# First block of a two-block network: decay rows by one product, small copies and half of the low weight parts on GpSimd, the solver's two problems joint, beta at the tokens

## The chip, the cores and the metric

The kernel runs on one core of a Trainium2 chip. The core has a matrix engine (TensorE, PE in the views), a vector engine (VectorE, DVE), a scalar engine (ScalarE, ACT), GpSimd (POOL) and SyncE (SP), which here issues nearly all transfers. Each engine takes its instructions in their order and waits on semaphores for the others. The metric is the device time of one execution in microseconds (us); lower is better.

## What is computed

The reference is a network of two blocks on 256 tokens of an input x and 256 of a context, with 1024 features. The change lies in the first block: a normalised and modulated input, one projection to queries, keys, values, decay and beta, gate and pooling inputs; then the gated delta rule in both directions over chunks of 64 tokens, with 8 heads of 128, beside a pooling branch. The part that matters, cut:

```python
def _gated_delta_rule(q, k, v, g, beta, s0):
    ...
    g = jnp.cumsum(g.reshape(bsz, nh, n, CHUNK), axis=-1)
    beta = beta.reshape(bsz, nh, n, CHUNK, 1)
    decay = jnp.exp(jnp.where(incl, g[..., :, None] - g[..., None, :], -jnp.inf))
    kb = k * beta
    a_mat = jnp.where(strict, jnp.einsum('bhncd,bhnsd->bhncs', kb, k) * decay, 0.0)
    rhs = jnp.concatenate([v * beta, kb * jnp.exp(g)[..., None]], axis=-1)
    sol = lax.linalg.triangular_solve(eye + a_mat, rhs, left_side=True, lower=True,
                                      unit_diagonal=True)
    ...
```

Per chunk, head and direction a unit triangular matrix of 64 x 64 is inverted. The pooling branch computes means over windows of one projection, subtracts, multiplies with a small matrix per group and gates the result.

## The kernel before

All products of weights are made in three float32r products (high by high, high by low, low by high). A weight arrives as a chunk of 2048 columns per partition (`wraw`), and is split in halves of 1024: the high part by ScalarE (`whl<-wraw`), the low part by VectorE (`whl<-wraw,whl`). Three raw buffers and two split ones rotate, so that a chunk is split while PE works on the chunk before it. The program is a list of steps; each step names its chunks, and the splits of a later step's chunk are put in as soon as a buffer is free. The order of the instructions on each engine is fixed when the program is built.

In the first block the stages are, in order of time:

- *Keys, decay and beta.* `rows_step` transposes the rows of log decay to tokens (`tk`), sums them along the chunk (`G`, and its negative `nG`), and makes beta by a reciprocal on VectorE (`abc`, rows 64 to 127). Beta goes to DRAM (`beta_d`).
- *Decay stage*, `gram_step`, one step per head. PE makes the products of keys (`ps_mm<-kv`), and per direction a bank with the mask (`ps_mm<-mskr,identr`) and the decay of the row's token spread over the partitions (`ps_mm<-cst,tk`, four float32 products of 128 columns). ScalarE takes the exponential (`gbuf<-ps_mm,nG`), VectorE multiplies the two (`gbuf<-ps_mm,gbuf`), and copies of the blocks go to `off` (64 rows) and `off32` (32 rows; both appear as `off` in the views). SyncE writes the diagonal blocks to DRAM (`lane_d`), and the decay (`dx_d`). The convolutions of the values (`vT`) lie between these on VectorE.
- *Values and inputs of the pooling branch* on PE: the last products of the values, then `u` and `zp` (one tile `uz`).
- *Solver*, on VectorE beside these. All diagonal blocks come back as lanes (`raw<-lane_d`): 128 partitions, each with two problems of 32 x 32. `X<-raw,bl` forms the negated matrix times beta, where `bl` is beta read back from DRAM by lanes; then 30 rounds of two operations for each of the two problems.
- *Pooling branch*: products `ps_mm<-hres,uz`, an eviction `wq`, its two parts `dp`, products `ps_fl<-dp,whl`.
- *Solver's output*, `solve_out`: six VectorE operations `O<-X,bl` multiply the inverses by beta and transpose some; they go to DRAM (`sol_d`) and come back as blocks (`Yw`, `TT`).
- *Inverses*: for two halves s of the chunks, the block below the diagonal by two rounds of 64 products of 32 x 32 (`ps_tr<-Yw,off`, `ps_tr<-TT,tmp`), between query products (`ps_fl<-hnx,whl`). Then the scan over the chunks (`ps_mm<-kv,TT` and so on) and the second block.

The lines that the text speaks of:

```python
                for c in range(4):
                    mm(gb[:, c * P:(c + 1) * P], tk[:, c, 32 * d + h:32 * d + h + 1].to_broadcast([P, P]), tri[d], False, c == 3)
...
                    nc.scalar.activation(out=T["off32"][q1, :, h, :], in_=at[q1, d, :, q2], func=AF.Copy)
...
                        nc.vector.tensor_tensor(out=c.lo[:, a:b], in0=c.raw[:, a:b], in1=c.hi[:, a:b], op=ALU.subtract)
```

Of the kernel before, what the change touches and what calls it, by code (L numbers as in the profile page):

```python
# [63 lines left out]
class Program:  # L64
    """Steps in their order, each with the weight pieces it uses; the pieces are loaded and split
    ahead of the steps, as far as there are buffers."""

    def __init__(self, tc):
        self.tc, self.nc = tc, tc.nc
        self.behind = self.behind_mods = ()  # L70
        self.split_to = 1 << 30
# [45 lines left out]
    def pump(self):  # L117
        nc = self.nc
        while True:
# [39 lines left out]
def adaln_net(ctx: ExitStack, tc: tile.TileContext, I, out):  # L159
# [1719 lines left out]
```

## Time and profile before

| what | value |
|---|---|
| three executions | 2118.60, 2118.64, 2121.05 us (median 2118.64) |
| profiled execution, its span | 2119.8 us |
| PE busy | 2077.7 us (98%) |
| DVE, ACT, POOL busy | 1266.4 (60%), 840.3 (40%), 77.4 us (4%) |
| decay stage on PE | 112.4 to 144.1 us |
| values, `u`, `zp` on PE | 144.1 to 223.0 us |
| solver on DVE | 159.65 to 232.8 us |
| scan's first products `ps_mm<-kv,TT` | from 288.8 us |

Times are microseconds from the start of the span. A row of a timeline gives start, duration, engine, line, operation, the tiles written and read, and how many alike stand in a row; in brackets the idle time before it and what ended it. A waiting time is put down to the event that came last.

### The profile page before, as it was taken

The numbers are of one execution on the slowest core, as the hardware profiler recorded it, in microseconds if no ns is written. First come the engines' busy times: TensorE is split into PE (matmuls) and PEld (weight loads), VectorE is DVE, ScalarE is ACT, GpSimd is POOL, SyncE is SP. The second block draws the span as 40 slices with busy tenths as digits, with TensorE's granted clock in tenths as the row PEclk, the third lists the DMA queues.
The fourth block names the chain that finished last, engine by engine and source line by source line (L and its number), as shares of the span: only waits on it lengthen the run. The fifth ranks groups of instructions, "written<-read, shape, count | busy, mean of one in ns | idle before, by whom it ended". The sixth has DMA issues, their size and how long they took to land.

```text
span 2119.8 us, 32648 instructions
## 1 busy us (share of the span) xinstructions
PE 2077.7 (98%) x13601; PEld 1797.6 (85%) x13601; DVE 1266.4 (60%) x2115; ACT 840.3 (40%) x1447; POOL 77.4 (4%) x80
## 2 busy tenths in 40 slices
PE   6999799999999999999999999999999999999999
PEld 6989798998788788888987878898888889579999
DVE  4669756578676764644766667466543236456553
ACT  4675362364322333433433233343322235555442
POOL 0000000030000002001000000110000010001000
PEclk9999999999999999999999999999999999999999
DMA  8243625544544443232244544324432233324453
GB/s 334 85 146 141 201 95 219 180 144 154 188 164 178 177 148 121 102 117 100 102 157 169 183 175 173 136 100 169 140 138 99 75 99 119 139 81 166 163 197 112
DMA packets 75379, 311.74 MB, mean 147 GB/s; under 512 B 26672, under 2 KB 36304, under 8 KB 45152
## 3 DMA queue, kind: packets, MB, share of 16 engines
q1 hardware_dynamic: 75232, 309.66, 41.5%
q8 instruction: 107, 1.75, 0.3%
q14 instruction: 40, 0.33, 0.0%
HBM read 301.72 MB, written 7.91 MB: 146 GB/s over the span
## 4 chain that ended last, share of the span: by engine, by line
PE 95%; DVE 2%; ACT 1%; DMA 1%; issue 1%; SPq 0%; ACTq 0%; DVEq 0%
PE ps_mm L218 61%; PE ps_fl L218 29%; PE ps_mod L218 3%; PE ps_tr L218 1%; PE ps_tr L234 1%; DVE O L240 0%; ACT gbuf L769 0%; DMA hres<-in_xT_dram 0%; DMA raw<-lane_d 0%; DVE X L237 0%; DVE gbuf L240 0%; ACT off L777 0%; PE ps_mm L234 0%; DVE vT L237 0%; DVE acc L240 0%
## 5 line engine op out<-in xcount | busy, mean ns | idle before, releaser
L218 PE MATMUL ps_mm<-hnh,whl 128*128 128x512 f32 (+1 forms) x2496 | 666.9, 351 | 1.1 <-ACT hnh L420 1.1
L150 ACT ACTIVATE whl<-wraw 128x1024 fp32r<-128x1024 f32 (+1 forms) x421 | 387.8, 970 | 592.3 <-PE ps_mm L218 192.4
L151 DVE TENSOR_TENSOR whl<-wraw,whl 128x1024 fp32r<-128x1024 f32 (+1 forms) x421 | 464.5, 1140 | 177.4 <-ACT whl L150 171.9
L218 PEld LDWEIGHTS ps_mm<-hnh,whl 128*128 128x128 f32 x2496 | 441.7, 190 | 67.2 <-issue 6.6
L218 PE MATMUL ps_mm<-hnl,whl 128*128 128x512 f32 (+1 forms) x1248 | 433.6, 349 | 0.0
L218 PE MATMUL ps_fl<-hnh,whl 128*128 128x512 f32 (+1 forms) x1040 | 292.3, 358 | 0.0
L237 DVE SCALAR_TENSOR_TENSOR macc<-wraw,cz,macc 128x512 f32<-128x512 f32 x392 | 268.1, 747 | 27.0 <-ACT macc L289 21.1
L218 PEld LDWEIGHTS ps_mm<-hnl,whl 128*128 128x128 f32 x1248 | 236.8, 190 | 28.9
L218 PE MATMUL ps_mm<-gh,whl 128*128 128x512 f32 (+1 forms) x924 | 243.6, 350 | 0.0
L218 PEld LDWEIGHTS ps_fl<-hnh,whl 128*128 128x128 f32 x1040 | 187.5, 189 | 30.3 <-issue 2.5
L218 PE MATMUL ps_fl<-hnl,whl 128*128 128x512 f32 (+1 forms) x520 | 185.2, 357 | 0.0
L218 PEld LDWEIGHTS ps_mm<-gh,whl 128*128 128x128 f32 x924 | 163.0, 189 | 23.0 <-issue 0.8
L218 PE MATMUL ps_mm<-gl,whl 128*128 128x512 f32 (+1 forms) x462 | 161.3, 349 | 0.0
L218 PE MATMUL ps_fl<-gh,whl 128*128 128x512 f32 (+1 forms) x616 | 159.5, 345 | 0.0
L240 POOL TENSOR_TENSOR nacc<-nacc,nsq 128x256 f32<-128x256 f32 x72 | 73.4, 1035 | 1597.0 <-ACT nsq L390 1455.0
L240 DVE TENSOR_TENSOR fg<-fs,ps_mm 128x512 f32<-128x512 f32 (+1 forms) x67 | 39.0, 584 | 154.5 <-PE ps_mm L218 146.5
L218 PEld LDWEIGHTS ps_fl<-gh,whl 128*128 128x128 f32 x616 | 107.5, 190 | 15.3 <-issue 1.6
L218 PEld LDWEIGHTS ps_fl<-hnl,whl 128*128 128x128 f32 x520 | 98.3, 189 | 13.5
L218 PE MATMUL ps_fl<-gl,whl 128*128 128x512 f32 (+1 forms) x308 | 105.5, 344 | 0.0
L218 PEld LDWEIGHTS ps_mm<-gl,whl 128*128 128x128 f32 x462 | 87.5, 189 | 11.1
L1296 ACT ACTIVATE fs<-ps_mm 128x512 f32<-128x512 f32 (+1 forms) x67 | 34.3, 514 | 136.1 <-PE ps_mm L218 136.0
L237 DVE SCALAR_TENSOR_TENSOR hres<-ps_mm,hg,hres 128x256 f32<-128x256 f32 x68 | 30.5, 480 | 81.5 <-PE ps_mm L218 81.4
(397 smaller groups left out, 2402.7 us busy)
## 6 DMA issues: line engine op xcount, KB each, us to landing
wraw<-in_ffn_up_dram SPq DMA_DIRECT2D x88, 1024.0 KB, 4.8
wraw<-in_w_mod_dram SPq DMA_DIRECT2D x72, 1024.0 KB, 4.8
wraw<-in_ffn_down_dram SPq DMA_DIRECT2D x64, 704.0 KB, 4.0
wraw<-in_sc_in_dram SPq DMA_DIRECT2D x12, 1024.0 KB, 4.7
wraw<-in_w_mod_a_dram SPq DMA_DIRECT2D x8, 1024.0 KB, 7.2
wraw<-in_w_out_dram SPq DMA_DIRECT2D x8, 1024.0 KB, 5.3
wraw<-in_w_k_dram SPq DMA_DIRECT2D x4, 1024.0 KB
wraw<-in_w_v_dram SPq DMA_DIRECT2D x4, 1024.0 KB, 4.7
```

The source lines that it names most:

```text
L150: nc.scalar.activation(out=c.hi[:, a:b], in_=c.raw[:, a:b], func=AF.Copy)
L151: nc.vector.tensor_tensor(out=c.lo[:, a:b], in0=c.raw[:, a:b], in1=c.hi[:, a:b], op=ALU.subtract)
L218: nc.tensor.matmul(out_, lhsT, rhs, start=start, stop=stop)
L234: nc.tensor.transpose(out_, in_, ident)
L237: return nc.vector.scalar_tensor_tensor(out=out_, in0=in0, scalar=scalar, in1=in1, op0=op0, op1=op1)
L240: return (eng or nc.vector).tensor_tensor(out=out_, in0=a, in1=b, op=op)
L1296: nc.scalar.activation(out=s_, in_=ps1[:, cols], func=AF.Silu)
```

## The change

- **Decay rows.** A new step `g_rows` transposes `nG` into rows once, splits them into a high part (rows 0 to 15, ScalarE) and a low part (rows 32 to 47, VectorE) of a tile `gt` that GpSimd clears first; it takes the memory of `tmp`. A selector `es` then spreads a row over the partitions by one float32r product of 512 columns per head and direction, in place of the four float32 products. `tk` and the products for `G` become smaller, and one transfer `eg_d` replaces two.
- **Small copies.** The 32 copies to `off32` move from ScalarE to GpSimd.
- **Low parts.** While the flag `share` is set, the second half of a chunk's low part is made by GpSimd.
- **Solver.** Both problems of a lane in one operation; `bl` is negated once on VectorE.
- **Beta at the tokens.** Beta is transposed to tokens (`bt`, `btz`) by PE and copied by VectorE. `solve_out` no longer multiplies: three ScalarE copies transpose, and six transfers go to `sol_d`, three of them straight from X. Beta is multiplied in by VectorE in the inverses: with the eviction `Z` (before by ScalarE), and behind the second round.

```diff
@@ pump
-                        nc.vector.tensor_tensor(out=c.lo[:, a:b], in0=c.raw[:, a:b], in1=c.hi[:, a:b], op=ALU.subtract)
+                        eng = nc.gpsimd if self.share and a else nc.vector
+                        eng.tensor_tensor(out=c.lo[:, a:b], in0=c.raw[:, a:b], in1=c.hi[:, a:b], op=ALU.subtract)
@@ rows_step, g_rows
+        tr = side_bank()
+        for c in range(4):
+            transpose(tr[:, c * P:(c + 1) * P], sg[:, c * P:(c + 1) * P])
+        T["bt"] = keep("bt", [P, 2, 4, 8])
+        nc.vector.tensor_copy(T["bt"], tr.rearrange("p (c i s) -> p i c s", c=4, s=32)[:, 2:4, :, 0:8])
...
+    def g_rows():
...
+        gt = T["gt"] = scr("tmp", [P, NT], 1, F32R)
+        nc.gpsimd.memset(gt.bitcast(F32), 0.0)
+        nc.scalar.activation(out=gt[0:16], in_=tr[0:16], func=AF.Copy)
+        tt(gt[32:48], tr[0:16], gt[0:16], ALU.subtract)
...
+        nc.scalar.activation(out=egs[0:16], in_=tr[0:16, 0:S], func=AF.Exp, scale=-1.0)
+        nc.sync.dma_start(out=eg_d.rearrange("d h t -> (d h) t"), in_=egs[0:16])
@@ gram_step
-                for c in range(4):
-                    mm(gb[:, c * P:(c + 1) * P], tk[:, c, 32 * d + h:32 * d + h + 1].to_broadcast([P, P]), tri[d], False, c == 3)
+                r = 8 * d + h
+                mm(gb, T["es"][:, r:r + 1].to_broadcast([P, P]), T["gt"], False, True)
...
-                    nc.scalar.activation(out=T["off32"][q1, :, h, :], in_=at[q1, d, :, q2], func=AF.Copy)
+                    nc.gpsimd.tensor_copy(out=T["off32"][q1, :, h, :], in_=at[q1, d, :, q2])
@@ solve_ops
+        nc.vector.tensor_scalar_mul(bl, bl, -1.0)
...
-            ts = [tmp[:, e * S:e * S + r * j].rearrange("p (a b) -> p a b", b=j) for e in range(2)]
-            for e, t in enumerate(ts):
-                tt(t, X[:, e, j + 1:32, j:j + 1].to_broadcast([P, r, j]), X[:, e, j:j + 1, 0:j].to_broadcast([P, r, j]), ALU.mult)
-            for e, t in enumerate(ts):
-                tt(X[:, e, j + 1:32, 0:j], X[:, e, j + 1:32, 0:j], t, ALU.add)
+            t = tmp[:, 0:2 * r * j].rearrange("p (e a b) -> p e a b", e=2, b=j)
+            n = [P, 2, r, j]
+            tt(t, X[:, :, j + 1:32, j:j + 1].to_broadcast(n), X[:, :, j:j + 1, 0:j].to_broadcast(n), ALU.mult)
+            tt(X[:, :, j + 1:32, 0:j], X[:, :, j + 1:32, 0:j], t, ALU.add)
@@ solve_out
-                    tt(O[e][f], X[f, e].rearrange("p a b -> p b a"), bl[f, q].unsqueeze(2).to_broadcast(one), ALU.mult)
-                    tt(O[e][w], X[w, e], bl[w, q].unsqueeze(2).to_broadcast(one), ALU.mult)
...
+        nc.scalar.activation(out=O2[w], in_=X[w, 1].rearrange("p a b -> p b a"), func=AF.Copy)
+        for e in range(2):
+            nc.scalar.activation(out=O[f, e], in_=X[f, e].rearrange("p a b -> p b a"), func=AF.Copy)
+        for e, a, b in ((2, X[f, 0], O2[w]), (0, O[f, 0], X[w, 0]), (1, O[f, 1], X[w, 1])):
+            for p, x in ((f, a), (w, b)):
+                nc.sync.dma_start(out=sol_d[e][p], in_=x.rearrange("p a b -> p (a b)"))
@@ steps
+    pr.add(lambda: setattr(pr, "share", True))
     for m in range(nv, H):
...
     pr.add(solve_out)
+    pr.add(lambda: setattr(pr, "share", False))
@@ inverses
-            nc.scalar.activation(out=Z.rearrange("p m t -> p (m t)"), in_=ps, func=AF.Copy)
+            tt(Z, ps.rearrange("p (m t) -> p m t", t=32),
+               T["btz"].rearrange("p c h -> p (c h)")[:, 2 * H * s:2 * H * (s + 1)].unsqueeze(2).to_broadcast([P, 2 * H, 32]), ALU.mult)
...
+            for d in range(2):
+                o = TT[:, d, 2 * H * s:2 * H * (s + 1), :]
+                tt(o, o, T["bt"][:, d].rearrange("p c h -> p (c h)")[:, 2 * H * s:2 * H * (s + 1)].unsqueeze(2).to_broadcast([P, 2 * H, 64]), ALU.mult)
```

The order of the instructions changes at three places. A row names the line, the operation, the tile written and those read, the shape and how many stand in a row.

VectorE where beta is made and the decay stage begins, before:

```order
L728 RECIPROCAL r_1243<-r_1243 64x512
L240 TENSOR_TENSOR gbuf<-ps_mm,gbuf 128x512 x2
L240 TENSOR_TENSOR abc<-abc,r_1243 64x512
L773 COPY off<-gbuf 64x4x64 x2
L240 TENSOR_TENSOR gbuf<-ps_mm,gbuf 128x512
L773 COPY off<-gbuf 64x4x64
L240 TENSOR_TENSOR gbuf<-ps_mm,gbuf 128x512
```

and with the change (`tmp` is the low part of the decay rows):

```order
L724 RECIPROCAL r_1236<-r_1236 64x512
L242 TENSOR_TENSOR abc<-abc,r_1236 64x512
L732 COPY bt<-ps_tr 128x64
L736 COPY btz<-bt 32x32 x4
L242 TENSOR_TENSOR tmp<-ps_tr,tmp 16x512
L816 TENSOR_SCALAR bl<-bl 128x64
L242 TENSOR_TENSOR gbuf<-ps_mm,gbuf 128x512
L795 COPY off<-gbuf 64x4x64
```

The first product `gbuf` now stands behind beta, its copies, the low part and the negation of `bl`, which is read from `beta_d`.

ScalarE where the inputs of the pooling branch end, before:

```order
L891 ACTIVATE uz<-ps_mm 128x256 x2
L150 ACTIVATE whl<-wraw 128x1024 x2
L891 ACTIVATE uz<-ps_mm 128x256 x3
L907 ACTIVATE wq<-ps_mm 128x256
L226 ACTIVATE dp<-wq 128x256
L907 ACTIVATE wq<-ps_mm 128x256
L226 ACTIVATE dp<-wq 128x256
```

and with the change:

```order
L908 ACTIVATE uz<-ps_mm 128x256 x2
L151 ACTIVATE whl<-wraw 128x1024 x2
L908 ACTIVATE uz<-ps_mm 128x256 x2
L842 ACTIVATE O_2621<-X 64x1024
L844 ACTIVATE O<-X 64x1024 x2
L908 ACTIVATE uz<-ps_mm 128x256
L924 ACTIVATE wq<-ps_mm 128x256
L228 ACTIVATE dp<-wq 128x256
```

The three copies of the solver's result stand ahead of the last `uz` and of the pooling branch's evictions `wq`.

VectorE at the end of the solver, before:

```order
L240 TENSOR_TENSOR tmp<-X 128x30 x2
L240 TENSOR_TENSOR X<-X,tmp 128x30 x2
L237 SCALAR_TENSOR_TENSOR uz<-ps_fl,vp,uz 128x256 x2
L240 TENSOR_TENSOR dp<-wq,dp 128x256 x2
L240 TENSOR_TENSOR mods_91<-ps_tr,vp 128x4 x2
L237 SCALAR_TENSOR_TENSOR uz<-ps_fl,vp,uz 128x256 x2
L240 TENSOR_TENSOR O_2708<-X,bl 64x1024 x2
L240 TENSOR_TENSOR O<-X,bl 64x1024 x4
L240 TENSOR_TENSOR dp<-wq,dp 128x256 x2
L237 SCALAR_TENSOR_TENSOR uz<-ps_fl,vp,uz 128x256 x2
```

and with the change:

```order
L242 TENSOR_TENSOR X<-X,tmp 128x2x3x28
L242 TENSOR_TENSOR tmp<-X 128x116
L153 TENSOR_TENSOR whl<-wraw,whl 128x1024
L242 TENSOR_TENSOR X<-X,tmp 128x2x2x29
L242 TENSOR_TENSOR tmp<-X 128x60
L242 TENSOR_TENSOR X<-X,tmp 128x2x30
L242 TENSOR_TENSOR dp<-wq,dp 128x256 x2
L153 TENSOR_TENSOR whl<-wraw,whl 128x1024
L239 SCALAR_TENSOR_TENSOR uz<-ps_fl,vp,uz 128x256 x2
L242 TENSOR_TENSOR dp<-wq,dp 128x256 x2
```

The six operations `O<-X,bl` are gone, the solver's last operation stands ahead of all `dp`, and one `whl` stands where two stood. GpSimd has ten `whl<-wraw,whl` of 128 x 1024 behind the 32 small copies, and two more behind its four settings `TT`.

## Rows read from the trace of the kernel before

**Rows 1.** Timeline of PE from 222 to 252 us: start, duration, instructions.

```profile
222.98 2.75 PE L218 MATMUL ps_mm<-hres,uz 128*128 128x256 f32 x12
...
249.56 2.50 PE L218 MATMUL ps_fl<-dp,whl 128*128 128x256 f32 x10 [9.38 <-DVE dp L240]
```

**Rows 2.** PE's waits, 96 to 300 us: total, times, longest.

```profile
PE ps_tr L218 <- issue: 3.9, 1, 3.9
```

**Rows 3.** Windows: length, busy time of PE, PEld, DVE, ACT, POOL, PEclk, DMA share, GB/s.

```profile
250.00:255.00 5.00, 4.85 (x23) 4.56 (x23) 2.93 (x4) 2.00 (x2) 0.00 (x0) 0.50 1.18 230
...
270.00:275.00 5.00, 5.00 (x25) 5.00 (x25) 1.13 (x3) 3.43 (x8) 0.00 (x0) 0.50 0.58 213
```

**Rows 4.** The chain of work that ended last, 110 to 290 us: start, duration, what.

```profile
151.86 7.77 DMA raw<-lane_d
...
269.84 7.42 PE ps_fl L218 x39
...
280.50 2.87 PE ps_fl L218 x24
```

**Rows 5.** Groups of instructions on PE, 188 to 226 us.

```profile
L218 PE MATMUL ps_mm<-hnx,whl 128*128 128x256 f32 x192 | 23.2, 283 | 0.0
```

**Rows 6.** Timeline of DVE, solver operations of 234 and of 30 elements.

```profile
209.78 0.71 DVE L240 TENSOR_TENSOR tmp<-X 128x234 f32<-128x234 f32 x2
...
232.52 0.31 DVE L240 TENSOR_TENSOR X<-X,tmp 128x30 f32<-128x30 f32 x2
```

**Rows 7.** Timeline of DVE, 113 to 122 us.

```profile
114.24 3.35 DVE L728 RECIPROCAL r<-r 64x512 f32<-64x512 f32 x1
117.62 1.29 DVE L240 TENSOR_TENSOR gbuf<-ps_mm,gbuf 128x512 f32<-128x512 f32 x2
118.94 0.69 DVE L240 TENSOR_TENSOR abc<-abc,r 64x512 f32<-64x512 f32 x1
```

**Rows 8.** Timeline of SyncE's queue, 117 to 165 us: issues.

```profile
125.22 0.74 SPq L793 DMA_DIRECT2D bl<-beta_d  x1
...
136.26 3.94 SPq L781 DMA_DIRECT2D lane_d<-gbuf  x6
```

**Rows 9.** Transfers, 110 to 260 us: issues, KB each, median us from issue to landing.

```profile
lane_d<-gbuf SPq DMA_DIRECT2D x32, 64.0 KB, 2.0
...
sol_d<-O SPq DMA_DIRECT2D x3, 512.0 KB, 2.6
...
Yw<-sol_d SPq DMA_DIRECT2D x4, 128.0 KB, 3.0
```

**Rows 10.** Groups of instructions, 112 to 148 us.

```profile
L769 ACT ACTIVATE gbuf<-ps_mm,nG 128x128 f32<-128x128 f32 x64 | 17.9, 376 | 3.8 <-PE ps_mm L218 3.0 <-ACT off L777 0.6
L218 PE MATMUL ps_mm<-cst,tk 128*128 128x128 f32 x128 | 16.8, 274 | 0.0
...
L777 ACT ACTIVATE off<-gbuf 32x128 f32<-32x128 f32 x28 | 8.5, 304 | 1.1 <-DVE gbuf L240 0.7
```

**Rows 11.** Groups of instructions on DVE, 159.6 to 232.9 us.

```profile
L151 DVE TENSOR_TENSOR whl<-wraw,whl 128x1024 fp32r<-128x1024 f32 x20 | 24.5, 1224 | 1.6 <-ACT whl L150 1.5
L237 DVE SCALAR_TENSOR_TENSOR X<-raw,bl 64x1024 f32<-64x1024 f32 x4 | 6.5, 1620 | 1.1 <-DMA raw<-lane_d 1.1
...
L240 DVE TENSOR_TENSOR dp<-wq,dp 128x256 fp32r<-128x256 f32 x4 | 1.7, 422 | 0.4 <-ACT dp L226 0.4
```

**Rows 12.** Timeline of DVE in the second block, 428 to 448 us.

```profile
428.04 2.36 DVE L151 TENSOR_TENSOR whl<-wraw,whl 128x1024 fp32r<-128x1024 f32 x2 [0.26 <-ACT whl L150]
...
431.24 6.73 DVE L151 TENSOR_TENSOR whl<-wraw,whl 128x1024 fp32r<-128x1024 f32 x4
```

**Rows 13.** Timeline of GpSimd, the same stretch.

```profile
434.47 0.74 POOL L240 TENSOR_TENSOR nacc<-nacc,nsq 128x256 f32<-128x256 f32 x1 [0.97 <-ACT nsq L390]
435.49 5.85 POOL L240 TENSOR_TENSOR nacc<-nacc,nsq 128x256 f32<-128x256 f32 x6 [0.27 <-ACT nsq L390]
```

**Rows 14.** Timeline of ScalarE, 186 to 200 us.

```profile
188.46 2.00 ACT L150 ACTIVATE whl<-wraw 128x1024 fp32r<-128x1024 f32 x2
```

More of the change, by code (lines that the diff above doesn't have):

```diff
@@ L75, in __init__ @@
         self.take, self.take_pool = 0, None
+        self.share = False
     def add(self, fn, *chunks, lead=False):
@@ L461, in new_scr, with keep @@
         T["scr"] = T["scr_ctx"].enter_context(tc.tile_pool(name=name, bufs=1))
-    def keep(tag, shape):
-        return T["pool"].tile(shape, F32, tag=tag, name=tag)
+    def keep(tag, shape, dt=F32):
+        return T["pool"].tile(shape, dt, tag=tag, name=tag)
     def big(tag, shape, dt=F32, name=None):
@@ L681, in run @@
                 nc.scalar.activation(out=T["v"][c // 2][:, c % 2, m, :], in_=tr[:, c * P:(c + 1) * P], func=AF.Copy,
-                                     scale=T["tk"][:, c, 64 + m:65 + m])
+                                     scale=T["tk"][:, c, 2, m:m + 1])
         return run
@@ L693, in rows_step @@
             transpose(tr[:, c * P:(c + 1) * P], rows[:, c * P:(c + 1) * P])
-        tk = T["tk"] = keep("tk", [P, 4, 72])
-        nc.scalar.activation(out=tk, in_=tr.rearrange("p (a b) -> p a b", a=4)[:, :, 0:72], func=AF.Copy)
-        load_table(AF.Exp, tk[:, 0, 0:1])
+        tk = T["tk"] = keep("tk", [P, 4, 3, 8])
+        nc.scalar.activation(out=tk, in_=tr.rearrange("p (a i s) -> p a i s", a=4, s=32)[:, :, 0:3, 0:8], func=AF.Copy)
+        load_table(AF.Exp, tk[:, 0, 0, 0:1])
         g = bank()
-        gl = g[:, 256:512]
         for d in range(2):
-            mm(g[:, d * P:(d + 1) * P], tri[d], tk[:, :, 32 * d:32 * d + 32])
+            mm(g[:, d * 32:(d + 1) * 32], tri[d], tk[:, :, d, :])
         for d in range(2):
-            mm(gl[:, d * P:(d + 1) * P], ones, tk[:, :, 32 * d:32 * d + 32])
+            mm(g[:, 64 + d * 32:96 + d * 32], ones, tk[:, :, d, :])
+        v4 = lambda x: x.rearrange("p (d c h) -> p d c h", d=2, h=8)
         G = scr("G", [P, 2, 4, 8])
-        nc.vector.tensor_copy(G, g[:, 0:256].rearrange("p (d c s) -> p d c s", d=2, s=32)[:, :, :, 0:8])
-        T["nG"] = keep("nG", [P, 2, 4, 8])
+        nc.vector.tensor_copy(G, v4(g[:, 0:64]))
+        T["nGs"] = keep("nG", [P, 4, 2, 8])
+        T["nG"] = T["nGs"].rearrange("p c d h -> p d c h")
         nc.vector.tensor_scalar_mul(T["nG"], G, -1.0)
-        glv = gl[:, 0:256].rearrange("p (d c s) -> p d c s", d=2, s=32)[:, :, :, 0:8]
+        glv = v4(g[:, 64:128])
         T["eG"] = keep("eG", [P, 2, 4, 8])
@@ L713, in rows_step @@
         nc.scalar.activation(out=T["eGl"], in_=glv, func=AF.Exp)
-        egs = scr("r0", [P, NT])[0:16, 0:S].rearrange("p (d t) -> p d t", d=2)
-        tr = side_bank()
-        for d in range(2):
-            transpose(tr[0:16, d * P:(d + 1) * P], G[:, d, 0:2, :].rearrange("p c h -> p (c h)"))
-        nc.scalar.activation(out=egs, in_=tr[0:16, 0:S].rearrange("p (d t) -> p d t", d=2), func=AF.Exp)
-        for c in range(2):
-            nc.sync.dma_start(out=eg_d[:, :, c * P:(c + 1) * P].rearrange("d h t -> h d t"), in_=egs[8 * c:8 * c + 8])
         tl = T["tail"] = keep("tail", [P, 2, 4, 8])
@@ L731, in rows_step @@
         nc.sync.dma_start(out=beta_d[8:16], in_=sg[96:104])
+        tr = side_bank()
[3 more added lines that the diff above has]
+        nc.vector.tensor_copy(T["bt"], tr.rearrange("p (c i s) -> p i c s", c=4, s=32)[:, 2:4, :, 0:8])
+        T["btz"] = keep("btz", [P, 4, 8])
+        for q in range(4):
+            p = slice(32 * q, 32 * q + 32)
+            nc.vector.tensor_copy(T["btz"][p], T["bt"][p, 1 - q % 2])
+    def g_rows():
+        tr = side_bank()
+        for c in range(4):
+            transpose(tr[0:16, c * P:(c + 1) * P], T["nGs"][:, c].rearrange("p d h -> p (d h)"))
+        gt = T["gt"] = scr("tmp", [P, NT], 1, F32R)
+        nc.gpsimd.memset(gt.bitcast(F32), 0.0)
+        nc.scalar.activation(out=gt[0:16], in_=tr[0:16], func=AF.Copy)
+        tt(gt[32:48], tr[0:16], gt[0:16], ALU.subtract)
+        es = T["es"] = keep("es", [P, 16], F32R)
+        tt(es, ident[:, 0:16], ident[:, 32:48], ALU.add)
+        nc.vector.tensor_scalar_mul(es, es.bitcast(F32), -1.0)
+        egs = scr("wq", [P, S], 2)
+        nc.scalar.activation(out=egs[0:16], in_=tr[0:16, 0:S], func=AF.Exp, scale=-1.0)
+        nc.sync.dma_start(out=eg_d.rearrange("d h t -> (d h) t"), in_=egs[0:16])
     def queued(step, key):
@@ L743, in adaln_net @@
     pr.add(lambda: new_scr("scr1b"))
+    pr.add(g_rows)
     lane_v = lane_d.rearrange("(d b c h) (r s) -> d b h r c s", d=2, b=2, h=8, s=64)
@@ L756, in run @@
                 T["gbuf"] = big("C", [P, 2, 2, 2, 4, P], name="gbuf")
-            kT, tk = T["kT"], T["tk"]
+            kT = T["kT"]
             gr = bank()
@@ L798, in solve_ops @@
             q = slice(32 * e, 32 * e + 32)
-            stt(X[f, e], raw[f, q, q].rearrange("p a b -> p b a"), -1.0, bl[f, q].unsqueeze(2).to_broadcast(one), ALU.mult, ALU.mult)
-            stt(X[w, e], raw[w, q, q], -1.0, bl[w, q].unsqueeze(1).to_broadcast(one), ALU.mult, ALU.mult)
+            tt(X[f, e], raw[f, q, q].rearrange("p a b -> p b a"), bl[f, q].unsqueeze(2).to_broadcast(one), ALU.mult)
+            tt(X[w, e], raw[w, q, q], bl[w, q].unsqueeze(1).to_broadcast(one), ALU.mult)
             yield 2.3
```

16 lines of the change are left out of this document (3 added, 13 removed).

## Prediction

> **What bounds the kernel now.** I read the granted clock by stretch first, then TensorE's waits, then the chain of work that ended last, and last the timelines of the engines that this chain passes through. TensorE (PE) is busy for 98% of the span. What it waits for in the part that the change touches, 110 to 290 us, is little and lies in one place: behind the pooling branch it stands 9.38 us, until VectorE has run six operations `O<-X,bl` and then splits the last `dp` [rows 1]. After that it stands 3.9 us in the inverses [rows 2], and the granted clock is 0.50, the lower of its two levels, in stretches behind both stands [rows 3]: 39 products that follow the second take 7.42 us, where 24 of the same form later take 2.87 [rows 4]. So about 17 us are to be had between 240 and 280 us, and next to nothing ahead of them: from 144 to 223 us PE runs products of 256 columns without a gap, 192 of them in 23.2 us or 0.121 us each, that is 5.8 us for a weight chunk of 48 [rows 5]. In the same stretch VectorE (DVE) is as full as PE: from the landing of `raw` (issued 151.86, landing after 7.77, so 159.6 [rows 4]) to the solver's last operation (232.8 [rows 6]) it hardly stops. Each part of the change has to be judged by whether it moves those two ends, PE's start at 144 and the solver's end.
>
> **The start of the decay stage.** Before, the first product `gbuf<-ps_mm,gbuf` ran at 117.62, right behind the reciprocal, and `abc` (beta) came later [rows 7]. Now the order on DVE is reciprocal, `abc`, the copies of beta, the low part of the decay rows, the negation of `bl`, and only then `gbuf`. Reciprocal end 117.6 plus 0.69 gives 118.3 for `abc`. Two writes of beta to DRAM and four reads `bl` back follow on SyncE's queue. An issue takes 0.74 [rows 8]; a small transfer lands after 2.0 (the nearest row is `lane_d` [rows 9]). That gives 118.3 + 2 x 0.5 + 2.0 = 121.3 for the write, 121.3 + 4 x 0.74 + 2.0 = 126.3 for the last `bl`, and 126.4 for the first `gbuf`: 8.8 later than before, between 6 (issues of 0.4) and 11 (landings of 3.0, the slowest of [rows 9]). Behind the waiting negation stand all the `gbuf` products, and behind these every `lane_d` write. The selector product must wait as well: GpSimd's clearing of the row tile, which reuses beta's memory, waits for the same write, then ScalarE's copy and DVE's subtraction; I put these near 123, so they are not the later branch.
>
> **The decay stage itself.** Gone from PE are 128 products `cst,tk`, 16.8 us busy, and from ScalarE 32 copies of 0.304 (28 of them in the row), 9.7 us; 16 products of 512 columns and 32 GpSimd copies come instead. ScalarE had 17.9 us of exponentials beside the copies [rows 10], 3.4 us per head, and the values' convolutions on top. Without the copies it is no longer the limit, but SyncE is close behind: four `lane_d` issues at 0.66 and a `dx_d`, taken the same, are 3.3 us per head [rows 8]. From the first `gbuf` to the issue of `raw` there were 34.2 us (117.62 to 151.86); eight heads at 3.3 and a landing of 2.0 are 28.4. I take that gain, 6, as the likely one; 2 if GpSimd, or DVE with the convolutions, holds a head at 3.8. Net: `raw`, and PE's dense stretch, start 2.8 us later; between 0 and +9.
>
> **The solver's stretch.** From 159.6 to 232.8 are 73 us. In it were 20 DVE operations `whl` at 24.5 us busy (some 1.16 each from start to start, as in [rows 12], 23 us), and four `X<-raw` of 1.62 that stay [rows 11]. Nine `whl` remain: 23 becomes 10.4. Four `dp` (1.7 us) and two `uz` of the same size now come behind the solver, 2.4 us in all, and the 1.6 us of waiting in the row of `whl` goes. The joint solver operations save nothing: two operations of 234 elements take 0.71 and two of 30 take 0.31 [rows 6], 0.98 ns per element and some 0.15 of start that the pair partly overlaps. One operation of twice the size has one start, but its successor needs its result: 60 x (0.19 + 0.98 x 0.330) = 31 us against 29. So 73 - 13 - 2.4 - 1.6 + 2 = 58 us, without GpSimd's effect.
>
> That effect is the disputed price. In the second block, where GpSimd adds squares of 256 elements, two `whl` on DVE take 2.36 but four that run beside GpSimd take 6.73 [rows 12]: 2.0 us lost, while some five GpSimd operations (0.74 alone, 0.98 in a row) fall in that time [rows 13]. So one of 256 costs a DVE operation with two SBUF inputs some 0.4 to 0.45. The moved halves have 1024 elements. Bounds: 0.45 if it is a price per instruction, 3.0 if DVE stops for the whole length (4 x 0.74). I scale by elements, 1.8, because the loss is more than half of the 0.74. Nine moved halves lie in the stretch, but the convolutions beside the first ones read PSUM, so I count seven: 12.6 us. X is ready at 159.6 + 2.8 + 58 + 12.6 = 233; so the work taken from DVE comes back as waiting, and the solver ends where it did. The page "SBUF — State Buffer" of the Trainium skill ("Who interferes with whom") speaks against the change here: a VectorE instruction with two SBUF inputs and a GpSimd one that reads SBUF exclude each other, and the loser blocks for the winner's whole length. The slowed `whl` agree in kind, 6.73 us for four against 2.36 for two. By the Trainium skill's "GPSIMD Engine Reference" (3.1) such an operation has some 2.6 cycles an element at 1.2 GHz, an estimate of 2.2 us for 1024, and with it the sum below would give 2115.5.
>
> PE itself can wait for GpSimd's halves, since each chunk needs one; a half is used some 12 products into its chunk and its slot came free a chunk before, 5.8 + 1.5 us, against two ScalarE halves of 1.0 [rows 14] and about 3 on GpSimd: covered by 2 us. If that cover goes, each further microsecond counts nine times.
>
> **The tail.** The 9.4 us of `O<-X,bl` leave DVE, and with them the stand. In their place ScalarE has three copies of X ahead of its last `uz` and of all evictions of the pooling branch: 233 + 3 x 1.0 = 236. Before, the pooling products began at 222.98, and without the stand would have ended at 249.56 + 1.2 - 9.4 = 241.4 [rows 1]; I put the first eviction at 224, so the branch needs 17.4 us behind it, of which PE can run some 1.9 ahead. It ends at 236 + 15.5 = 251.5, where before it ended at 250.8: +0.7. The tail's round trip through DRAM, 236 + 0.7 + 2.6 + 4 x 0.74 + 3.0 = 245 [rows 8, 9], is by then over; it was what stretched the first products `Yw,off`. Behind it fall away the 3.9 us (the eviction of the first inverse product moves from ScalarE, which stood behind a transfer, to DVE), about 2.4 of low clock in 250 to 255 and 7.42 - 39 x 0.121 = 2.7 later [rows 3, 4], and some 1.0 of gaps: -10. New on the path are two multiplications of 1024 by beta behind the second inverse, 2 x 1.2 = +2.4. Sum: 0.7 - 10 + 2.4 = -6.9; after the scan's start nothing differs. For the transfers of `sol_d`, six instead of three on an idle queue, I count nothing. The 16.8 us of `cst,tk` that go from PE are worth nothing further, since other engines limit the stage.
>
> The profiled span, 2119.8, lies 1.2 above the median of 2118.64 and inside the runs' spread (2118.60 to 2121.05); -6.9 from the median, with one allowed for collisions of the last two GpSimd halves with the inverses' multiplications, is -5.9: **2112.7 us**.
>
> **Rivals.** (a) *GpSimd costs little* (0.45 each): X at 224; then PE sets the pace and the branch ends at 241.4 + 2.8, 6.6 ahead of before; -6.6 - 10 + 2.4 = -14: 2104.5. For it: the 0.45 of the row is certain, the scaling is not. Chance 0.25. (b) *GpSimd stops DVE for its whole length, in all nine*: 26.6 us, X at 247, the branch ends near 265, +14.5 - 7.6 = +7: 2125.5. DVE is then what the chunks wait for, since 1.14 + some six solver operations (3.4) + 3.0 is over PE's 5.8. It decides from X = 240 on, that is 2.2 us a half if all nine count; past 244 (2.6 a half) the kernel is slower by over 0.2%. The Trainium skill's lock is this rival's reason. Chance 0.20. (c) *The late start stays and the clock falls*: PE stands some 8 us at 114 to 122, and behind a stand of 9.4 the clock was 0.50 up to 255 [rows 3]; the heads then go by PE, perhaps 1.5 us more for three of them, +4: 2117. Against it: small products remain in that gap. Chance 0.15. (d) The forecast, X between 230 and 239: 0.40.
>
> **How the numbers follow.** A difference under 0.2% (4.2 us) can't be told from no change. The forecast's own range is 2109 to 2117, three quarters of it past 0.2%; (a) is all faster, (b) slower for the most part, the rest same, (c) mostly same. With something for prices that no row shows, faster 0.50, same 0.29, slower 0.21. The range reaches to (a), 2103, and short of (b)'s end, 2124.
>
> **What would show it.** First `gbuf` on DVE near 126 and `raw` issued near 154.5 (right), near 120 and 148 (the read back is cheaper). `whl` or solver operations near 2.5 to 3 us long beside GpSimd's `whl` of 2.2 to 4. X ready near 233; O copies on ScalarE right behind it; no stand of 9 us at the end of pooling; the clock at 1.00 from 245 to 280. The prediction is wrong if PE waits for GpSimd's `whl` chunk by chunk, if ScalarE stands over 5 us at the O copies, or if the first `gbuf` comes without the wait for `bl`.

## The result: 2131.7 us, slower by 0.56%

The changed kernel takes 2131.66 us in the median of four runs (2130.47 to 2135.32), the kernel before 2119.85 beside them; the ratio is 1.0056, with a 95% interval of 1.0044 to 1.0069. The forecast was 2112.7, faster. The profiled execution of the changed kernel has a span of 2131.0 us, 11.2 longer than that of before.

**Where PE waits now**, 96 to 310 us (its waits: total, times, longest):

```profile
PE ps_mm L220 <- DVE whl L153: 4.8, 5, 1.5
PE ps_mm L220 <- ACT uz L908: 4.5, 1, 4.5
PE ps_tr L236 <- DVE abc L242: 4.3, 1, 4.3
PE ps_tr L236 <- ACT vT L674: 3.8, 1, 3.8
```

The stand of 9.4 us behind `O<-X,bl` [rows 1] is gone, as forecast. In its place stand 4.8 us in five waits for VectorE's `whl`, 3.8 for `vT`, 4.5 for the last `uz` and 4.3 for `abc`. From 96 us to the pooling branch PE had waited for 4.2 us in all before.

To see what each stage lost I took the time between the first PE instructions of neighbouring stages from both traces. The table is worked out from their start times, and the last column is for comparison with a run below (the change without GpSimd's halves):

```
us from first to first                          before    after   without halves
transposes of the rows to first value product     33.8     37.0     37.0
... to first product of u                         31.5     36.9     33.0
... to first product of zp                        24.3     25.9     24.3
... to first product of the pooling branch        23.0     27.3     23.0
... to ps_mm<-q,kv in the scan                   124.6    119.5    121.6
... to the end                                  1772.2   1776.3   1774.6
```

The decay stage costs 3.2 more, the three stages beside the solver 11.3 more, the tail gives 5.1 back. The last line holds work whose order the change does not touch but for its beginning; it varied by 4 us over all the runs here (1772 to 1776). Against that the first line begins 2.3 us earlier, so about 2 us of the 11 between the two profiles are not the change's.

**The chain that ended last** tells which engine set the pace in these stages. One row of it before, then five with the change (start, duration, what):

```profile
188.94 36.79 PE ps_mm L218 x297
```

```profile
191.87 2.69 DVE whl L153
...
210.75 2.75 DVE X L242
...
231.38 2.48 DVE tmp L242
...
237.19 1.98 ACT O L842
239.20 3.75 ACT O L844 x2
```

Before, the chain runs on PE from 171 to 239 us. With the change it runs for the most part on VectorE from 163 us, where `raw` lands, to 237 us, and then through the three copies of X on ScalarE to 243 us.

**GpSimd** (timeline of the changed kernel, 150 to 220 us):

```profile
153.56 2.44 POOL L153 TENSOR_TENSOR whl<-wraw,whl 128x1024 fp32r<-128x1024 f32 x1 [4.89 <-ACT whl L151]
...
166.28 4.18 POOL L153 TENSOR_TENSOR whl<-wraw,whl 128x1024 fp32r<-128x1024 f32 x1 [10.29 <-ACT whl L151]
...
190.77 2.71 POOL L153 TENSOR_TENSOR whl<-wraw,whl 128x1024 fp32r<-128x1024 f32 x1 [3.33 <-DVE vT L239]
...
210.52 2.46 POOL L153 TENSOR_TENSOR whl<-wraw,whl 128x1024 fp32r<-128x1024 f32 x1 [4.78 <-ACT whl L151]
```

**VectorE** in the same stretch:

```profile
154.03 3.10 DVE L239 SCALAR_TENSOR_TENSOR vT<-ps_mm,vp,vT 128x508 f32<-128x508 f32 x4 [0.30 <-ACT vT L594]
...
162.95 8.59 DVE L242 TENSOR_TENSOR X<-raw,bl 64x1024 f32<-64x1024 f32 x4 [2.92 <-DMA raw<-lane_d]
...
183.97 1.22 DVE L153 TENSOR_TENSOR whl<-wraw,whl 128x1024 fp32r<-128x1024 f32 x1
...
191.80 2.77 DVE L153 TENSOR_TENSOR whl<-wraw,whl 128x1024 fp32r<-128x1024 f32 x1
...
209.38 0.66 DVE L242 TENSOR_TENSOR X<-X,tmp 128x480 f32<-128x480 f32 x1
...
210.75 2.74 DVE L242 TENSOR_TENSOR X<-X,tmp 128x476 f32<-128x476 f32 x1
```

The two are read side by side. (SBUF holds the tiles; PSUM holds the `ps_` banks that PE writes its products to.) A half takes GpSimd 2.4 to 2.8 us where it has its turn at once. The VectorE operation with two SBUF inputs that falls behind its start is longer by 1.6 to 2.2 us: an operation of 480 elements takes 0.66, but the one of 476 at 210.75, beside GpSimd's half of 210.52, takes 2.74; a `whl` takes 2.77 instead of 1.22. The other way round, GpSimd's half of 166.28 started beside VectorE's `X<-raw` and took 4.18, while the four of these took 8.59 instead of the 6.5 of [rows 11]. In these rows it is one operation after the other, not both at once. The four `vT` beside the half of 153.56, which read PSUM, keep their length (3.10 us for four).

Each of the nine halves between 160 and 237 us holds up one such operation; together, worked out from the timeline against the length of the same or the nearest operation undisturbed, they cost VectorE 18.3 us.

**The solver's end** (timelines of the changed kernel, VectorE and then ScalarE):

```profile
236.93 0.22 DVE L242 TENSOR_TENSOR X<-X,tmp 128x60 f32<-128x60 f32 x1
243.96 0.43 DVE L242 TENSOR_TENSOR dp<-wq,dp 128x256 fp32r<-128x256 f32 x1 [6.80 <-ACT dp L228]
```

```profile
237.19 1.98 ACT L842 ACTIVATE O<-X 64x1024 f32<-64x1024 f32 x1 [4.28 <-DVE X L242]
239.20 3.75 ACT L844 ACTIVATE O<-X 64x1024 f32<-64x1024 f32 x2
242.86 0.36 ACT L908 ACTIVATE uz<-ps_mm 128x256 f32<-128x256 f32 x1
243.12 0.36 ACT L924 ACTIVATE wq<-ps_mm 128x256 f32<-128x256 f32 x1
```

X is ready at 237.15, and the three copies take 1.98, 1.9 and 1.9 us before the last `uz` and the first `wq` of the pooling branch can leave PSUM at 242.9 and 243.1.

**The start of the decay stage** (timeline of VectorE, then windows, columns as in [rows 3]):

```profile
111.78 3.35 DVE L724 RECIPROCAL r<-r 64x512 f32<-64x512 f32 x1
115.17 0.69 DVE L242 TENSOR_TENSOR abc<-abc,r 64x512 f32<-64x512 f32 x1
...
119.07 0.68 DVE L242 TENSOR_TENSOR tmp<-ps_tr,tmp 16x512 fp32r<-16x512 f32 x1 [0.68 <-ACT tmp L745]
122.04 0.20 DVE L816 TENSOR_SCALAR bl<-bl 128x64 f32<-128x64 f32 x1 [2.29 <-DMA bl<-beta_d]
122.15 0.68 DVE L242 TENSOR_TENSOR gbuf<-ps_mm,gbuf 128x512 f32<-128x512 f32 x1
```

```profile
116.00:119.00 3.00, 2.05 (x8) 1.00 (x8) 1.25 (x5) 0.55 (x1) 0.52 (x1) 0.50 0.06 11
...
128.00:131.00 3.00, 2.23 (x13) 1.45 (x11) 2.93 (x6) 2.75 (x9) 1.03 (x4) 1.00 0.45 125
```

The program reached this stage 2.3 us earlier than before, a difference that its first 100 us show from run to run. Counted from the copy of `G` on VectorE, the first `gbuf` comes after 12.1 us, where it came after 5.0 (117.62 in [rows 7]), and PE's transposes of beta wait 4.3 us for `abc`. In that stand the granted clock falls: it is 0.50, the lower level, from 113.5 to 127.2 us.

### The profile page after: what moved, and what is told of

It is laid out like the page before. It is cut to its first block, busy times and chain, and to the rows that moved or that the text cites. A ratio compares the mean times of both kernels' runs of the same rounds, so it can differ in the third digit from the quotient of the medians.

```text
span 2131.0 us, 32438 instructions
## 1 busy us (share of the span) xinstructions
PE 2076.4 (97%) x13495; PEld 1788.0 (84%) x13495; DVE 1267.4 (59%) x2052; ACT 836.6 (39%) x1417; POOL 120.7 (6%) x125
## 4 chain that ended last, share of the span: by engine, by line
PE 92%; DVE 5%; ACT 2%; DMA 1%; issue 1%; SPq 0%; DVEq 0%; ACTq 0%
PE ps_mm L220 58%; PE ps_fl L220 29%; PE ps_mod L220 3%; DVE X L242 1%; DVE tmp L242 1%; DVE whl L153 1%; PE ps_tr L220 1%; DVE vT L239 1%; PE ps_tr L236 1%; ACT gbuf L791 0%; DMA raw<-lane_d 0%; DMA hres<-in_xT_dram 0%; ACT whl L151 0%; DVE nt L239 0%; PE ps_mm L236 0%
## 5 line engine op out<-in xcount | busy, mean ns | idle before, releaser
L153 DVE TENSOR_TENSOR whl<-wraw,whl 128x1024 fp32r<-128x1024 f32 (+1 forms) x409 | 451.2, 1140 | 177.5 <-ACT whl L151 172.3
L220 PEld LDWEIGHTS ps_fl<-hnl,whl 128*128 128x128 f32 x520 | 98.4, 189 | 13.7
L1318 ACT ACTIVATE fs<-ps_mm 128x512 f32<-128x512 f32 (+1 forms) x67 | 34.3, 513 | 138.0 <-PE ps_mm L220 137.9
```

The source lines that it names most:

```text
L153: eng.tensor_tensor(out=c.lo[:, a:b], in0=c.raw[:, a:b], in1=c.hi[:, a:b], op=ALU.subtract)
L220: nc.tensor.matmul(out_, lhsT, rhs, start=start, stop=stop)
L1318: nc.scalar.activation(out=s_, in_=ps1[:, cols], func=AF.Silu)
```

## Experiments

All were timed in three rounds beside the kernel before. Lengths of stages are differences of starts in the traces, as in the table.

**1. The change without GpSimd's halves.**

```diff
-    pr.add(lambda: setattr(pr, "share", True))
```

> The change without GpSimd's halves (all low parts on VectorE again). Theory A, GpSimd's operations stop VectorE for their whole length, some 2.2 us each, and so set PE's pace from 166 to 237 us: the 11 us that PE lost there are won back, 2117 to 2122, no VectorE operation of 60 to 480 elements is over 0.7 us long, and X is ready near 232. Theory B, the loss comes from where the new instructions stand (copies of X on ScalarE ahead of the evictions, beta ahead of the decay stage): no more than 3 us faster than the changed kernel, 2128 or more.

Measured: 2121.25 us, ratio to the kernel before 1.0006 (0.9996 to 1.0016). So the halves cost some 10 us here, as theory A says; the rest of the change together is worth nothing. The chain that ended last is back on PE, with the same 297 products as before:

```profile
190.45 36.78 PE ps_mm L220 x297
```

The groups of VectorE's instructions (160 to 237 us) show the operations at their old length, in this run and then in the changed kernel:

```profile
L242 DVE TENSOR_TENSOR X<-raw,bl 64x1024 f32<-64x1024 f32 x4 | 6.5, 1622 | 2.9 <-DMA raw<-lane_d 2.9
...
L242 DVE TENSOR_TENSOR tmp<-X 128x480 f32<-128x480 f32 x2 | 1.3, 656 | 0.0
```

```profile
L242 DVE TENSOR_TENSOR X<-X,tmp 128x476 f32<-128x476 f32 x2 | 5.5, 2740 | 0.1
```

VectorE has 20 `whl` again in that stretch instead of 9, and yet X is ready at 235.0 and not at 237.2 (theory A had expected 232). One thing else changes with this edit: in the order that is built here the first six `wq` stand ahead of the copies of X, which start at 235.07. The 10 us are therefore not the halves' alone by this run; runs 3, 4 and 11 bear on that.

**2. The kernel before with GpSimd's halves alone.**

```diff
-                        nc.vector.tensor_tensor(out=c.lo[:, a:b], ..., op=ALU.subtract)
+                        eng = nc.gpsimd if self.share and a else nc.vector
+                        eng.tensor_tensor(out=c.lo[:, a:b], ..., op=ALU.subtract)
```

> The kernel before with GpSimd's halves alone. Theory A: ten halves that stop VectorE by 2.2 us each, less 1.15 us of VectorE's own work each, put the solver some 8 to 12 us later, but the solver's end is not ahead of the pooling branch here, so PE loses only where a chunk's first half is late: 2122 to 2130. Theory B: within 3 us of the kernel before, 2116 to 2122.

Measured: 2144.56 us, 1.0118 (1.01 to 1.0136): slower by 24 us, more than twice the most that either theory gave (2130). PE's longest wait, GpSimd's timeline and VectorE's beside it:

```profile
PE ps_mm L220 <- POOL whl L153: 16.0, 2, 8.0
```

```profile
185.99 16.06 POOL L153 TENSOR_TENSOR whl<-wraw,whl 128x1024 fp32r<-128x1024 f32 x2 [3.53 <-DVE vT L239]
209.32 2.44 POOL L153 TENSOR_TENSOR whl<-wraw,whl 128x1024 fp32r<-128x1024 f32 x1 [7.27 <-ACT whl L151]
215.07 15.35 POOL L153 TENSOR_TENSOR whl<-wraw,whl 128x1024 fp32r<-128x1024 f32 x2 [3.32 <-ACT whl L151]
```

```profile
196.80 0.71 DVE L242 TENSOR_TENSOR tmp<-X 128x240 f32<-128x240 f32 x2
208.27 1.23 DVE L153 TENSOR_TENSOR whl<-wraw,whl 128x1024 fp32r<-128x1024 f32 x1 [10.76 <-ACT whl L151]
```

Two GpSimd operations take 16.06 us in a row (the first alone 13.7), and two more 15.35, where a lone one takes 2.4. VectorE runs out of solver operations at 197.5, and only then does GpSimd come through: its second operation ends at 202.05, 4.5 us or two operations later. PE stands until the first is done. VectorE's operations of this solver come in pairs that do not need each other, a pair every 0.63 us; GpSimd does not get a turn between them.

**3. The halves and the joint solver** (run 2's edit and this one), to test that.

```diff
...
-                tt(t, X[:, e, j + 1:32, j:j + 1].to_broadcast([P, r, j]), X[:, e, j:j + 1, 0:j].to_broadcast([P, r, j]), ALU.mult)
+            tt(t, X[:, :, j + 1:32, j:j + 1].to_broadcast(n), X[:, :, j:j + 1, 0:j].to_broadcast(n), ALU.mult)
...
```

> The kernel before with GpSimd's halves and the joint solver. With the halves alone GpSimd needed 8 us for two of its operations, and 2144.6 was the time. Theory A, GpSimd gets its turn only when VectorE leaves a gap, and the joint operations, each of which needs the one before, leave one after each: GpSimd's operations take 2.4 to 2.9 us again, and the time is 2126 to 2134. Theory B, the 8 us had another cause (a late high part, a transfer): they stay, and the time is over 2138.

Measured: 2130.83 us, 1.005 (1.0032 to 1.0069). Theory A holds; GpSimd's timeline:

```profile
194.01 2.40 POOL L153 TENSOR_TENSOR whl<-wraw,whl 128x1024 fp32r<-128x1024 f32 x1 [4.68 <-ACT whl L151]
...
206.43 2.41 POOL L153 TENSOR_TENSOR whl<-wraw,whl 128x1024 fp32r<-128x1024 f32 x1 [3.52 <-ACT whl L151]
```

No operation is over 3.5 us. So the joint solver, which saves nothing itself (run 4), is what makes the halves bearable. That GpSimd gets its turn because each joint operation waits for the one before is the likely reading, but not the only one: the joint operations are also twice as long (480 elements against 240), and no run separates the two. PE still waits 4.5 us for `whl` and 3.3 for `vT`, and the chain that ended last runs on VectorE here too. The halves cost 11 us against the kernel before and 9 against run 4, from which this run differs by them alone; neither has the copies of X.

**4. The joint solver alone.**

> The kernel before with the solver's two problems joint, nothing else. Theory A (by the rows, 31 us of solver operations against 29): VectorE ends 1 to 3 us later, which the pooling branch hides, 2117 to 2122. Theory B, a joint operation saves starts: up to 3 us faster, 2115 to 2117.

Measured: 2121.96 us, 1.001 (0.9996 to 1.0023): no difference, in theory A's range.

**5. Beta at the tokens alone** (with the smaller products for the sums of the decay, for memory).

```diff
-            nc.scalar.activation(out=Z.rearrange("p m t -> p (m t)"), in_=ps, func=AF.Copy)
+            tt(Z, ps.rearrange("p (m t) -> p m t", t=32), T["btz"]..., ALU.mult)
```

> The kernel before with beta at the tokens alone (copies of X on ScalarE, six transfers, beta in the inverses), and with the smaller products for the decay's sums, which its memory needs. Both theories take the six multiplications off VectorE. If the stand of 9.4 us goes and the round trip is hidden, 10 to 14 us faster than before, 2105 to 2109; if the two transposing copies on ScalarE (some 1.9 us each, as in the changed kernel) and the multiplications in the inverses eat it, 2114 to 2119.

Measured: 2113.89 us, 0.9969 (0.9956 to 0.9982), 6.7 us faster than before, just below the second of the two ranges. In the profile (span 2109.3) the pooling branch to the scan is 10.7 shorter. PE's waits, 230 to 300 us:

```profile
PE ps_fl L218 <- ACT dp L226: 1.6, 1, 1.6
PE ps_mod L218 <- ACT Yw L951: 1.6, 2, 1.1
PE ps_tr L218 <- ACT TT L1002: 1.1, 1, 1.1
```

The stands of 9.4 and 3.9 us are gone, and 4.3 us in four waits take their place. Here the scheduler put ScalarE's copies behind most of the branch's evictions.

**6. The decay rows by one product alone.**

```diff
-                    mm(gb[:, c * P:(c + 1) * P], tk[:, c, 32 * d + h:32 * d + h + 1].to_broadcast([P, P]), tri[d], False, c == 3)
+                mm(gb, T["es"][:, r:r + 1].to_broadcast([P, P]), T["gt"], False, True)
```

> The kernel before with the decay rows by one product alone (copies still on ScalarE, beta still behind the first products). Theory A: the later first exponential (some 6 us) costs as much as the shorter heads give back, 2117 to 2123. Theory B, PE's stand and the lower clock behind it cost more than that: 2124 or more.

Measured: 2130.38 us, 1.0044 (1.003 to 1.0059), slower by 10, theory B. VectorE's and PE's timelines:

```profile
113.59 3.35 DVE L722 RECIPROCAL r<-r 64x512 f32<-64x512 f32 x1
...
120.83 0.68 DVE L240 TENSOR_TENSOR tmp<-ps_tr,tmp 16x512 fp32r<-16x512 f32 x1 [3.17 <-ACT tmp L734]
```

```profile
121.57 1.22 PE L218 MATMUL ps_mm<-tmp,es 128*128 128x512 f32 x2 [7.86 <-DVE tmp L240]
```

PE stands 7.86 us before the first selector product: the low part waits for ScalarE, ScalarE for GpSimd's clearing, and that for beta's write from the same memory, which stands behind the reciprocal. The stage is 5.9 us longer than before.

**7. The rows made ahead of the reciprocal**, in memory of their own; low parts on VectorE, solver as before, beta at the tokens, small copies on GpSimd.

```diff
+        gt = T["gt"] = big("X", [P, NT], F32R, name="gt")
+        nc.gpsimd.memset(gt.bitcast(F32), 0.0)
+        a = nc.scalar.activation(out=gt[0:16], in_=tr[0:16], func=AF.Copy)
+        b = tt(gt[32:48], tr[0:16], gt[0:16], ALU.subtract)
...
         T["behind"] = (a.ins, b.ins)
         with pr.queued(T["behind"]):
             rr = scr("r1", [P, NT])
```

> The changed kernel with all low parts on VectorE, the solver as before (so no negation of bl), and the decay rows made ahead of the reciprocal, in memory of their own. Theory A, the decay stage lost by its late start alone (reciprocal ahead of the low part, clearing behind the write of beta, and the lower clock that followed): the first exponential comes within 2 us of its place before, the clock stays at 1.00, the stage is 3 to 6 us shorter than before, and with the tail's gain the time is 2106 to 2112. Theory B, the stage is limited by another engine per head: no shorter than before, 2112 to 2116.

Measured: 2111.77 us, 0.9961 (0.9949 to 0.9973). The late start is repaired: the first exponential stands 5.6 us behind the rows' transposes, where it stood 4.3 before and 12.6 in the change. But the stage is 34.3 us long against 33.8: one product for four is worth nothing. The time lies in the range of theory A, but theory A's signs are missing (the stage is no shorter, the clock does not stay at 1.00), and the length of the stage speaks for theory B. Windows of this run:

```profile
116.00:122.00 6.00, 4.67 (x18) 3.75 (x18) 5.63 (x9) 2.93 (x10) 0.00 (x0) 0.50 0.28 81
...
134.00:140.00 6.00, 5.38 (x18) 4.14 (x18) 5.20 (x11) 2.78 (x10) 2.42 (x8) 0.53 0.54 161
```

The clock was at 0.50 and 0.53 in two of these windows without any long stand, and VectorE is busy for 5.6 and 5.2 of their 6 us.

**8. The same with zero products**, to see whether the clock is the reason.

```diff
+                for c in range(4):
+                    mm(gb[:, c * P:(c + 1) * P], T["zc"].to_broadcast([P, P]), tri[d], False, False)
```

> The run with the early rows, and in each bank of the decay stage four float32 products of 128 columns with a column of zeros, which add nothing to the sums: PE has as many products there as before the change. Theory A, the stage was no shorter because PE, less busy, got the lower clock (0.50 in two stretches of it): the clock stays at 1.00 in the stage although PE does more, and PE's values begin at the same time or up to 3 us earlier than with the early rows alone; the whole 2108 to 2113. Theory B, the lower clock cost nothing and other engines set the heads: the clock at 1.00 and the values later by 1 to 4 us, 2113 to 2116; or the clock falls all the same.

Measured: 2121.05 us, 1.0001 (0.9992 to 1.0011).

```profile
116.00:122.00 6.00, 4.87 (x35) 4.38 (x36) 5.81 (x8) 2.76 (x12) 0.00 (x0) 1.00 0.24 70
...
134.00:140.00 6.00, 5.86 (x44) 5.24 (x43) 5.31 (x11) 3.58 (x13) 1.84 (x6) 1.00 0.29 72
```

The clock is at 1.00 throughout, and the stage is 3.3 us longer (37.6): theory B, though the time is 5 us above its range. (Of the rest of the difference to run 7, 3.2 us lie in the tail and 2.6 in work that is the same in both.) The products bring the clock back, but the lower clock had cost less than the products do; what it cost by itself this run can't tell, since it changes both. What limits the stage with few products I did not single out; VectorE, full in the middle heads, is the candidate.

**9. Beta at the tokens and the small copies on GpSimd.**

```diff
-                    nc.scalar.activation(out=T["off32"][q1, :, h, :], in_=at[q1, d, :, q2], func=AF.Copy)
+                    nc.gpsimd.tensor_copy(out=T["off32"][q1, :, h, :], in_=at[q1, d, :, q2])
```

> Beta at the tokens (as in the run with the tail alone) and the small copies on GpSimd, all else as before. If ScalarE's copies were what limited a head (3.9 us of which 1.2 are copies), the decay stage is 2 to 4 us shorter and the time 2109 to 2112; if PE's 128 products or VectorE limit it as well, nothing changes and the time is 2112 to 2116.

Measured: 2110.66 us, 0.9959 (0.9946 to 0.9971), the best here and 0.0010 from the tail alone, whose interval overlaps. The time is in the first range, but the decay stage is 33.7 us long, as before, so the copies were not what limited a head.

**10. That run with the copies of X on VectorE.**

```diff
-        nc.scalar.activation(out=O2[w], in_=X[w, 1].rearrange("p a b -> p b a"), func=AF.Copy)
+        nc.vector.tensor_copy(out=O2[w], in_=X[w, 1].rearrange("p a b -> p b a"))
```

> The run with beta at the tokens and the small copies on GpSimd, with the three copies of X on VectorE. There the copies take 1.9 to 2.0 us each on ScalarE and PE waits 1.7 us for a part of dp behind them. If ScalarE's copies still cost those 1.7 us, 1 to 2 us faster than that run (2109 to 2110); if VectorE's own work behind them (uz, dp) is as late, no change, 2110 to 2113.

Measured: 2116.72 us, 0.998 (0.997 to 0.999), 4.5 us slower by the ratios than with ScalarE. The 1.7 us behind `dp` go, but PE then stands 7.9 us in two waits in the inverses; neither expectation had this, and the profile shows nothing that PE waited for in them, so why is open. The copies themselves are faster there: 1.1 us each on VectorE, 2.0 on ScalarE.

**11. The changed kernel with the copies of X on VectorE.**

> The changed kernel whole, with the three copies of X on VectorE, which is idle for 6.8 us there, in place of ScalarE. If the place of the copies ahead of the pooling branch's evictions cost what PE waited there (4.5 us), 3 to 5 us faster than the changed kernel, 2127 to 2129; if the branch waits for VectorE's dp behind the copies instead, no change, 2130 to 2133.

Measured: 2131.99 us, 1.0057 (1.0042 to 1.0072): no change. PE's wait there only has another name:

```profile
PE ps_mm L220 <- ACT wq L924: 5.9, 1, 5.9
```

The three copies take 3.1 us on VectorE, and the first two `dp` follow at 241.4, with no wait of PE for them in the profile. What the late `wq` (251.07) stands behind is a split of weights on ScalarE, and this behind a transfer (timeline of ScalarE, then a row of the chain that ended last):

```profile
249.16 2.00 ACT L151 ACTIVATE whl<-wraw 128x1024 fp32r<-128x1024 f32 x2 [6.87 <-DMA wraw<-in_w_q_dram]
```

```profile
239.56 9.53 DMA wraw<-in_w_q_dram
```

The transfer is issued 1.9 us after the `whl` of 236.40 on VectorE ends, and behind the first two writes of X to `sol_d` on SyncE's queue; in the changed kernel it is issued at 238.40, in the same place, and ScalarE waits for it until 247.65. Before, SyncE had issued the first of the chunks of `in_w_q_dram` at 221.32. So with the copies out of the way the branch still waits for work that stands behind VectorE's late operations, which is why their place on ScalarE is worth nothing here.

## Why the prediction was wrong

**The step that failed** is the price of GpSimd's halves: "I count seven: 12.6 us", and with it the cover in "PE itself can wait for GpSimd's halves ... covered by 2 us". All nine halves held up VectorE, for 18.3 us together, among them those beside the convolutions; so X came 74.2 us after `raw`, where the forecast had 70.6. And I let the price move only the solver's end. VectorE's queue also holds the `whl` and `vT` that PE needs: the values, `u` and `zp` lost 11.3 us where the forecast had none, and the chain that ended last moved from PE to VectorE. Run 1 gives 10 us back without the halves, and run 3 against run 4 puts them at 9.

This is the mechanism of rival (b), all nine halves at nearly GpSimd's whole length; only its 3.0 us each was too much. Its arithmetic had the stall (1.14 + 3.4 + 3.0 is over PE's 5.8), but I gave it 0.20. A half that holds up one solver operation makes the next `whl` late, since a static order puts five to nine solver operations between two `whl`.

X alone does not carry the miss: with X at 237.15 the forecast's own sum would still give about 2117. The rest, worked out from the traces: 2.7 for the copies of X, 2.6 for the branch behind its first eviction (18.1 us, not 15.5), which the inverses give back, and some 11 behind the scan's first products, where the forecast says that "nothing differs". There 25 query products, 3 us, come that had run ahead of the scan before, the clock is at 0.50 for 3.4 us from 298, and 4.1 lie in the last line of the table, which varies by as much.

**The price of one half.** The scaling by elements came close: 1.8 us forecast, 2.0 measured per half, which is near GpSimd's whole operation. X was due at 233 and came at 237.2. The rule of the page "SBUF — State Buffer" of the Trainium skill ("Who interferes with whom"), that the later of the two blocks for the whole length of the first, is what the timelines show (2.74 us for an operation of 0.65 us). In run 2 GpSimd waited for much longer than one operation of VectorE.

**The decay stage.** Net +2.8 was forecast for `raw` and for the values' start. The stage on PE measured +3.2, which is near by luck, since both terms were off and the path was another one; counted from the copy of `G`, `raw` was issued 4.8 later. The first `gbuf` came 7.1 us later, not 8.8: beta's round trip was shorter. The rows' own chain, which I called "not the later branch", was nearly as late (the first four exponentials end at 121.8, the first `gbuf` starts at 122.15), and run 6 shows that it is late without the negation of `bl` too. The heads gave back less than 6: from the first `gbuf` to the issue of `raw` 32.0 us passed, against 34.2, a gain of 2.2. Rival (c), the lower clock at the start, was seen as described; its price is not singled out, since run 8 brings the clock back only with products that cost more.

**The copies of X** were priced by the row of a contiguous `whl`, 3 x 1.0 [rows 14]; they read X transposed and took 5.7. That term was mis-sized by 2.7. The six `O<-X,bl` were a warning: with a mean of 1.54, three took 1.2 and three 1.9. It did not hold for every form, though: as plain copies on VectorE the same three took 1.0 to 1.1 (runs 10 and 11).

**The tail.** Forecast from the branch's start to the scan: -9.4 of stand, -10 of waits and clock, +2.4. Alone it gave 10.7 in the profile and 6.7 in the time (run 5), and in the changed kernel 5.1. The copies of X ahead of the evictions are not shown to be the reason: in run 1, where most evictions stand ahead of them, it is 2.9, and in run 11, without them on ScalarE, 3.5. Why this stretch gains less beside the other parts is open. Alone, the mechanism was right and the size off: new waits of 0.5 to 1.6 us took the place of those removed. The joint solver (no gain) was as forecast.

So the change is, roughly, a gain of 7 (beta at the tokens), nothing from the joint solver and the small copies, a loss of some 7 to 10 from the late rows (what run 1 leaves for them, and run 6) and of 9 to 11 from GpSimd's halves. Runs 5, 7 and 9 keep the first and leave or repair the others: 0.3 to 0.4% faster than before, with the same computation and with intervals that overlap. Run 9 has the lowest time.

## What to carry to other kernels

Work that was moved to GpSimd beside a VectorE that is full cost VectorE 1.6 to 2.2 us for each GpSimd operation of 2.4 to 2.8, wherever VectorE's operation had both inputs in SBUF; the convolutions that read PSUM kept their length. In a static order, price a slower engine at every instruction that another engine waits for, not at the end of its queue. Before a product is saved, find what limits the stage: here PE's 128 products lay beside work that took as long.

## What the runs showed of the hardware that was not expected

- GpSimd can starve: against back-to-back VectorE operations that do not depend on each other, two GpSimd operations of 2.4 us took 16.1 us; with the joint operations, which are twice as long and depend on each other, each took 2.4 to 3.5 (runs 2 and 3).
- The granted clock fell to 0.50 in a stage where PE was busy for 3.8 to 5.6 us in each 6 and never stood longer than 1.9 us (run 7); with products of zeros in the same stage it stayed at 1.00 (run 8).
- A ScalarE copy of 64 x 1024 that reads transposed takes 1.9 to 2.0 us (the changed kernel), where a contiguous one of 128 x 1024 takes 1.0 [rows 14]; on VectorE the same transposing copies take 1.0 to 1.1 (runs 10 and 11).
